# Split weight slabs of the gates: written to memory in the second token block, not in the first

## Chip, cores and metric

The kernel runs on one core of a Trainium2 chip. The metric is the device time of one launch in microseconds (us), given as the median of the runs that were made.

## The reference, cut to what matters

One layer of a streaming encoder. For 2048 prompt tokens and 64 sample tokens, with D_MODEL = 1024:

```python
h = rms_norm(x, norm1_g) * (1 + sc1) + sh1
z = h @ w_in                      # columns: glu_a, glu_b | q, k, v | g_conv, g_attn
u = glu_a * sigmoid(glu_b)
conv_out = swish(layer_norm(depthwise_conv31(u))) @ w_conv_out
attn_out = band_attention(rms_norm(q), rms_norm(k), v) @ w_attn_out   # 8 heads of 64
merged = sigmoid(g_conv) * conv_out + sigmoid(g_attn) * attn_out
x = x + gt1 * (merged @ w_o)
x = x + gt2 * swiglu_ffn(rms_norm(x, norm2_g) * (1 + sc2) + sh2)
```

The gates of this text are `g_conv` and `g_attn`: 2048 of the columns of `w_in`. All numbers are 32-bit floats.

## The kernel before, in words

**Products in three parts.** A 32-bit operand is split into a rounded part `hi`, a copy by the ScalarE (ACT) to the type float32r, and the rest `lo = src - hi`, a subtraction by the VectorE (DVE) or the GpSimd engine (POOL). `mm3` (L700) then makes three matmuls for each product: hi*hi, hi*lo and lo*hi. Weights have to be split as well. Their raw slabs are loaded into tiles named `wst`, their parts are the tiles `whi` and `wlo`.

**Two phases.** The first phase computes everything from `h` to the two mixers, in four blocks of tokens (`PBLOCKS`: 576 tokens, then three times 512). The second phase merges, projects and runs the FFN in three larger blocks. This text is about the first phase. There, for each block b, the stages follow in the order q, conv column 0, k, conv column 1, v, conv columns 2 and 3, g (`ORDER`, L553); the g stage computes the gates from 16 slabs of 512 rows by 256 columns, 512 KB each, in 8 pairs (`gates`, L1315). The key of such a slab is `("in", column, half)`, with three entries; the slabs of the conv columns have keys `("in", column)`, with two.

**Weights that come back.** The same weight slabs are needed in each of the four blocks. In block 0 a slab is loaded raw, split, and its two parts are stored to memory (`w_din_h`, `w_din_l`, 512 KB each, L501). In blocks 1 to 3 the two parts are loaded from there (L466). The first four slabs, those of q, are treated otherwise: block 0 doesn't store them (`passing`), and block 1 loads them raw once more, splits them and stores them.

**Who orders the work.** The class `Weights` keeps up to 5 split slabs (`held`) and, once opened, 3 raw ones (`staging`). `split` (L451) is called for the next slab as soon as an older one has been given back; `load` (L368) fetches the next raw slab as soon as a raw tile has been split. A small planner (`Stream`) adds up an estimated load of each engine and starts side work (norms of the next block, the attention heads, the convolution, its layer norm) in lanes between the matmuls, when their due times come. The framework then orders the instructions of each engine by its own estimate of when each can run. At run time each engine, and the SyncE queue (SP) that issues nearly all DMAs, works through its list in order.

**Engines in the first phase.** In block 0 DVE makes `wlo` for all slabs with `in` keys, POOL or DVE for others; in the second phase POOL makes most of them. DVE also runs the depthwise convolution, 31 taps as `y <- u, wd, y`, which lags behind the conv stages and reaches into the g stage of its block, and its part of the attention (`pr`, `sm`, `pl`). POOL runs sums of the layer norm (`s`, `y`), the reciprocal root (`r`) of the norms and small copies. The rows of the next block come as `x_t` (L1121), are squared by ACT (`junk`), scaled by DVE with POOL's `r`, and turned by the PE (`pt <- ident, x_t`) before the next block can begin on them.

Of the kernel before, what the change touches and what calls it, by code (L numbers as in the profile page):

```python
# [84 lines left out]
class Meter:  # L85


    def __init__(self, engine, name, stream):
        self.engine, self.name, self.stream = engine, name, stream
# [174 lines left out]
class Weights:  # L264
# [5 lines left out]
    def __init__(self, engines, pool, dram, stream, keys, source, staging, held, kept):  # L270
        self.stream = stream
        self.sync, self.act, self.dve, self.gps = engines
        self.pool, self.dram, self.keys, self.source = pool, dram, keys, source

        self.staging, self.held, self.reach = staging, held, 0
        self.sum_pool, self.sum_d, self.sums, self.hold, self.landed = None, None, {}, 0, {}
        self.behind = nullcontext

        self.room, self.leaving = {"wst": 1, "wup": 0, "wfo": 0}, {"wst": 0, "wup": 0, "wfo": 0}
        times, raws = {}, {}  # L280
        self.items, self.users, self.need, self.first, self.stored, self.spread = [], [], {}, set(), {}, set()

        def item(key):
            self.items.append(key)
            self.users.append(0)
            return len(self.items) - 1

        for i, key in enumerate(keys):
            n = times[key] = times.get(key, 0) + 1
            if key[0] == "up" and n == 1:  # L290
                self.first.add(i)
                cs = [c for f, op in key[1:] for c in self.columns_of(f, op)]
                for c in cs:
                    if c not in raws:
                        raws[c] = item(("fi", c))
                self.need[i] = sorted({raws[c] for c in cs})
                for f, op in key[1:]:
                    for c in self.parts_of(f, op):
                        self.users[raws[c]] += 1
            elif key[0] == "dn":  # L300
                fs = [key[:3], (*key[:2], key[2] + 1)]
                for f in fs:
                    if f not in raws:
                        raws[f] = item(("fo", f[2]))
                self.need[i] = [raws[f] for f in fs]
                for op in key[3:]:
                    for e in self.rows_of(op):
                        self.users[raws[fs[e]]] += 1
            elif n == 1 or not kept(key) or n == 2 and key[:2] == ("qkv", 0):
                self.need[i] = [item(key)]  # L310
                self.users[self.need[i][0]] += 1
                if key[0] == "fo" and key[1] in last_rows(0) and n == 1:
                    self.spread.add(self.need[i][0])
        self.raws = raws
        self.again = {key for key, n in times.items() if n > 1 and kept(key)}
        self.loaded, self.ready, self.used, self.freed, self.given = {}, [], 0, 0, 0

        self.extra = {"wst": staging - 1, "wup": 1, "wfo": 2}

        self.tags = {"fo": (), "": ("wst", "wup", "wfo")}  # L320
        self.due = {kind: [] for kind in self.tags}
        for i, key in enumerate(self.items):
            self.due[self.kind(key)].append(i)
        self.load_on("")
# [126 lines left out]
    def split(self):  # L451
        i = len(self.ready)
        key = self.keys[i]
        its = self.need.get(i, ())
        if key[0] == "dn":
            shape = [P, len(key) - 3, 512]
        elif i in self.first:
            shape = [P, 4 * len(key) - 4, P]
        else:
            shape = list(self.loaded[its[0]][0].shape) if its else self.stored[key][1]  # L460
        hi = self.pool.tile(shape, F32R, tag="whi", name="whi", bufs=self.held)
        lo = self.pool.tile(shape, F32R, tag="wlo", name="wlo", bufs=self.held)
        self.ready.append((hi, lo))
        if not its:
            for t, d in zip((hi, lo), self.stored[key][0]):
                self.sync.dma_start(t.bitcast(F32), d)  # L466
            return
        turn = {"wo": key[1], "fi": key[1] // P if key[0] == "fi" else 0}.get(key[0], 0)

        passing = key[:2] == ("qkv", 0) and i < 4  # L470
        on_dve = key[0] == "in" or key[0] == "qkv" and (passing or key[1]) or turn % 2
        if key[0] == "dn":
            parts = [(slice(j, j + 1), self.second(key, op)) for j, op in enumerate(key[3:])]
            self.stream.after("act", "pool")
        elif i in self.first:
            parts = [(slice(4 * j, 4 * j + 4), self.operand(f, op)) for j, (f, op) in enumerate(key[1:])]
            self.stream.after("act", "pool")
        else:
            n = 4 if key[0] == "fi" else shape[1]
            parts = [(slice(j, j + n), self.loaded[its[0]][0][:, j : j + n]) for j in range(0, shape[1], n)]  # L480
        for c, src in parts:

            late = key[0] in ("up", "fo") and self.stream.load["pool"] - self.stream.load["pe"] > POOL_BEHIND
            e, name = (self.dve, "dve") if on_dve or late else (self.gps, "pool")
            self.act.activation(hi[:, c], src, AF.Copy)
            self.stream.after(name, "act")
            e.tensor_tensor(lo[:, c], src, hi[:, c].bitcast(F32), ALU.subtract)
        if i in self.first:
            its = [self.raws[c] for f, op in key[1:] if op[0] == "a" for c in self.parts_of(f, op)]
        if key[0] == "dn":  # L490
            its = [self.raws[*key[:2], key[2] + int(op[1]) - 1] for op in key[3:] if op[0] == "b"]
        for j in its:
            self.drop(j, name)
        if key[0] == "dn" and key[3] == "b11":
            self.sum_second(key)

        def then():
            if key in self.again and key not in self.stored and not passing:
                ds = [self.dram.tile(shape, F32, name="w_d" + "_".join(map(str, key)) + "_" + part) for part in "hl"]
                for t, d in zip((hi, lo), ds):  # L500
                    self.sync.dma_start(d, t.bitcast(F32))  # L501
                self.stored[key] = ds, shape
            self.presum()

        self.stream.at(self.stream.when(name), then, True)

    def there(self, i):
# [56 lines left out]
def seven(s, f):  # L564


    return s > 0 and 2 <= f < NF - 2


def last_rows(s):  # L570

    return range(NF - (2 if s else 4), NF)


DOWN_OPERANDS = (("b11", "b21"), ("t3", "t2"), ("t1", "t4"), ("b22",))


def mod_order():
# [5 lines left out]
def weight_order():  # L584
# [10 lines left out]
    for s in range(len(CBLOCKS)):  # L595
# [4 lines left out]
        for f in range(0, NF, 2):  # L600
            ops = up_operands(f) + up_operands(f + 1)
            for j in range(0, len(ops), 2):
                yield ("up", *ops[j : j + 2])
                if f >= 2 and seven(s, f - 2):
                    yield from (("dn", s, f - 2, *DOWN_OPERANDS[i]) for i in {0: (0,), 2: (1, 2), 4: (3,)}.get(j, ()))
                elif j == 0 and f >= 2 and f - 2 not in last_rows(s):
# [5 lines left out]
def streaming_layer(ctx: ExitStack, tc: tile.TileContext, I, O):  # L612
# [1189 lines left out]
    for s, (lo, hi) in enumerate(CBLOCKS):  # L1802
# [215 lines left out]
        def down_pair(f):  # L2018
# [9 lines left out]
            def products(pss, a, w, j, first, last, i, e):  # L2028
                for p in range(n):
                    c = slice(p * P, p * P + P)  # L2030
                    mm3(pss[p], a[0][:, c], a[1][:, c], w[0][:, j], w[1][:, j], first, last, skip_group_check=True)
                    stream.after("dve", "pe")
                    dst = acc[p + i * n][:, 512 * e : 512 * e + 512]
                    dve.tensor_tensor(dst, dst, pss[p], ALU.add)

            w = W.get(("dn", s, f, *DOWN_OPERANDS[0]))
            products(ys, a11, w, 0, True, False, 0, 0)
# [3 lines left out]
            W.done()  # L2041
            w = W.get(("dn", s, f, *DOWN_OPERANDS[1]))
            products(zs, s3, w, 0, True, False, 1, 1)
            yield
            products(ys, s2, w, 1, False, False, 1, 0)
            W.done()
            w = W.get(("dn", s, f, *DOWN_OPERANDS[2]))
            products(ys, s1, w, 0, False, False, 1, 1)
            products(zs, a22, w, 1, False, True, 1, 0)
            W.done()  # L2050
            yield
            w = W.get(("dn", s, f, *DOWN_OPERANDS[3]))
            products(ys, s4, w, 0, False, True, 0, 1)
# [201 lines left out]
```

## Time and profile before

| | |
|---|---|
| median of 3 runs | 2989.11 us (2988.55 to 2995.56) |
| span of the profiled execution, first to last instruction | 2982.2 us |
| PE (matmul) busy | 2906.6 us, 97% |
| DVE, ACT, POOL busy | 2047.4, 1363.6, 1165.8 us (69%, 46%, 39%) |
| DMA, mean over the span | 211 GB/s |
| g stage of block 0, as far as its gate instructions show | about 195 to 332 us |
| g stage of block 1 | about 504 to 622 us |

The profile names no other time for its execution than the span; the median of the runs lies 6.9 us above it, which is what lies before the first and after the last instruction, and the difference between one execution and another. Times inside the span count from its first instruction. "Busy" of the PE counts overlapping matmuls, so a busy PE need not be at its peak. All lines of a helper carry its number, so that most instructions show L102; they are told apart by the names of their tiles.

### The profile page before, as it was taken

What the parts mean: (1) busy time and instruction counts of PE and PEld (TensorE: products, weight loads), DVE (VectorE), ACT (ScalarE), POOL (GpSimd) and SP (SyncE); (2) the same over time, 40 slices, a digit from 0 to 9 for tenths busy, and PEclk for the clock granted to TensorE, in tenths of its full rate; (3) what the DMA queues carried; (4) which work ended last, traced back from release to release, by engine and by line L of the source; (5) the groups of instructions that cost most, each with busy time, mean ns of one, the idle gap of its engine ahead of it and who ended that gap; (6) DMA issues with size and microseconds to landing.
All of it is one profiled execution on the core that took longest, in us unless ns stands there. A gap on an engine that the chain in (4) does not pass through costs nothing. (4 is left out here: it accounts for less than half of the span.)

```text
span 2982.2 us, 44930 instructions
## 1 busy us (share of the span) xinstructions
PE 2906.6 (97%) x16241; PEld 2588.0 (87%) x16241; DVE 2047.4 (69%) x3628; ACT 1363.6 (46%) x2459; POOL 1165.8 (39%) x752
## 2 busy tenths in 40 slices
PE   7999899999999999989999999999999999999999
PEld 4899777787888888878989899999999999999998
DVE  5897687667857885477677755676666557566666
ACT  3345643662456257464443335544444345444442
POOL 0201310111011102444666443365766742465767
PEclk9999999999999999999999999999999999999999
DMA  8989889888997888885444786423333975333333
GB/s 296 304 282 306 264 286 312 279 256 276 308 283 221 281 256 277 265 284 167 139 147 149 233 268 222 135 89 113 114 106 116 308 244 184 98 96 114 114 104 126
DMA packets 467724, 628.06 MB, mean 211 GB/s; under 512 B 36276, under 2 KB 314664, under 8 KB 467501
## 3 DMA queue, kind: packets, MB, share of 16 engines
q1 hardware_dynamic: 453456, 605.58, 62.8%
q10 hardware_dynamic: 14045, 19.60, 1.9%
q8 instruction: 128, 2.10, 0.3%
q14 instruction: 95, 0.78, 0.1%
HBM read 476.53 MB, written 148.54 MB: 210 GB/s over the span
## 5 line engine op out<-in xcount | busy, mean ns | idle before, releaser
L102 PE MATMUL ps<-t,whi 128*128 128x384 f32 (+1 forms) x2112 | 502.7, 322 | 9.5 <-ACT t L102 4.9
L102 POOL TENSOR_TENSOR wlo<-wst,whi 128x1024 fp32r<-128x1024 f32 (+1 forms) x160 | 365.1, 2292 | 254.1 <-ACT whi L102 231.9
L102 ACT ACTIVATE whi<-wst 128x1024 fp32r<-128x1024 f32 (+1 forms) x264 | 257.4, 977 | 324.8 <-PE ps L102 118.5
L102 PE MATMUL ps<-b,whi 128*128 128x384 f32 (+1 forms) x1584 | 381.3, 326 | 6.1 <-DVE early L102 3.4
L102 PEld LDWEIGHTS ps<-t,whi 128*128 128x128 f32 x2112 | 367.6, 188 | 17.2 <-ACT t L102 5.1
L102 DVE SCALAR_TENSOR_TENSOR y<-u,wd,y 128x512 f32<-128x512 f32 (+1 forms) x480 | 369.1, 773 | 6.4
L102 PE MATMUL ps<-hh,whi 128*128 128x512 f32 (+2 forms) x992 | 361.3, 364 | 0.0
L102 DVE TENSOR_TENSOR acc<-acc,pd 128x512 f32<-128x512 f32 (+1 forms) x482 | 322.5, 685 | 54.9 <-PE pd L102 52.4
L102 PE MATMUL ps<-hl,whi 128*128 128x512 f32 (+2 forms) x992 | 345.2, 348 | 0.0
L102 PE MATMUL ps<-hh,wlo 128*128 128x512 f32 (+2 forms) x992 | 344.9, 348 | 0.0
L102 PE MATMUL ps<-t,wlo 128*128 128x384 f32 (+1 forms) x1056 | 339.3, 321 | 1.0 <-POOL wlo L102 0.7
L102 PE MATMUL pd<-whi,hid 128*128 128x512 f32 (+1 forms) x956 | 307.2, 391 | 0.2 <-DVE hid L102 0.2
L102 PEld LDWEIGHTS ps<-b,whi 128*128 128x128 f32 x1584 | 278.6, 189 | 12.4 <-DVE early L102 4.2
L102 POOL TENSOR_TENSOR r<-t,mhalf 128x1 f32<-128x1 f32 (+3 forms) x68 | 83.7, 1232 | 456.4 <-DVE t L102 451.3
L102 PE MATMUL ps<-b,wlo 128*128 128x384 f32 (+1 forms) x792 | 256.9, 325 | 0.0
L102 ACT ACTIVATE pr<-pr,sm 128x640 f32<-128x640 f32 (+3 forms) x272 | 200.2, 747 | 109.7 <-DVE sm L102 107.1
L102 PEld LDWEIGHTS pd<-whi,hid 128*128 128x128 f32 (+1 forms) x956 | 174.6, 183 | 42.4 <-ACT hid L102 0.7
L102 PEld LDWEIGHTS ps<-hh,wlo 128*128 128x128 f32 x992 | 186.6, 188 | 21.7
L102 PEld LDWEIGHTS ps<-hh,whi 128*128 128x128 f32 x992 | 187.2, 189 | 18.5 <-issue 1.6
L102 PEld LDWEIGHTS ps<-hl,whi 128*128 128x128 f32 x992 | 187.3, 189 | 15.5 <-issue 1.4
L102 PEld LDWEIGHTS ps<-t,wlo 128*128 128x128 f32 x1056 | 198.2, 188 | 2.6 <-POOL wlo L102 1.3
L102 POOL TENSOR_TENSOR wlo<-ws,whi 128x512 fp32r<-128x512 f32 x96 | 125.2, 1325 | 173.7 <-ACT whi L102 170.8
(227 smaller groups left out, 6307.0 us busy)
## 6 DMA issues: line engine op xcount, KB each, us to landing
whi<-w_din_h SPq DMA_DIRECT2D x72, 512.0 KB, 6.6
wlo<-w_din_l SPq DMA_DIRECT2D x72, 512.0 KB, 8.2
wst<-sum_d SPq DMA_DIRECT2D x132, 256.0 KB, 2.8
wfo<-in_w_ffn_out SPq DMA_DIRECT2D x64, 512.0 KB, 3.3
wmod<-in_w_ada SPq DMA_DIRECT2D x46, 512.0 KB, 6.2
sum_d<-ws SPq DMA_DIRECT2D x88, 256.0 KB, 2.4
wst<-in_w_ffn_in SPq DMA_DIRECT2D x84, 256.0 KB, 3.1
wst<-in_w_in SPq DMA_DIRECT2D x40, 512.0 KB, 9.1
```

Of the source, the lines that this page charges most:

```text
L102: self.last = f(*args, **kw)
```

## The change

In block 0 the 16 gate slabs are loaded raw and split as before, with `lo` on DVE, but are not stored. In block 1 they are loaded raw again, split once more, now with `lo` on POOL, and the two parts are stored. Blocks 2 and 3 load the stored parts as before. The sets `unkept` and `anew` hold the positions in the list of weights of the first and of the later uses of these slabs.

```diff
@@ Weights.__init__
+        self.anew, self.unkept = set(), set()
...
         for i, key in enumerate(keys):
             n = times[key] = times.get(key, 0) + 1
+            if gate_slab(key):
+                (self.anew if n > 1 else self.unkept).add(i)
...
-            elif n == 1 or not kept(key) or n == 2 and key[:2] == ("qkv", 0):
+            elif n == 1 or not kept(key) or n == 2 and (key[:2] == ("qkv", 0) or gate_slab(key)):
                 self.need[i] = [item(key)]
@@ Weights.split
-        on_dve = key[0] == "in" or key[0] == "qkv" and (passing or key[1]) or turn % 2
+        on_dve = key[0] == "in" and i not in self.anew or key[0] == "qkv" and (passing or key[1]) or turn % 2
...
         def then():
-            if key in self.again and key not in self.stored and not passing:
+            if key in self.again and key not in self.stored and not passing and i not in self.unkept:
@@
+def gate_slab(key):
+
+    return key[0] == "in" and len(key) == 3
```

## The prediction

> **What bounds the kernel now.** I read the page first, then the busy time by windows of the two g stages, then who ended the waits of PE.
>
> ```profile
> PE 2906.6 (97%) x16241; PEld 2588.0 (87%) x16241; DVE 2047.4 (69%) x3628; ACT 1363.6 (46%) x2459; POOL 1165.8 (39%) x752
> ```
> ```profile
> core 0: us, PE busy (x) PEld busy (x) DVE busy (x) ACT busy (x) POOL busy (x), PEclk, DMA share, GB/s
> 195.00:332.00 137.00, 132.84 (x968) 127.64 (x967) 105.48 (x221) 81.22 (x182) 24.91 (x23) 1.00 0.86 282
> 504.00:622.00 118.00, 114.38 (x617) 96.56 (x616) 83.76 (x167) 70.75 (x130) 12.71 (x13) 1.00 0.90 286
> 504.00:549.00 45.00, 44.38 (x223) 36.80 (x221) 42.23 (x77) 21.94 (x39) 2.36 (x3) 1.00 0.89 281
> 549.00:622.00 73.00, 70.00 (x394) 59.76 (x395) 41.52 (x90) 48.80 (x91) 10.35 (x11) 1.00 0.91 288
> 352.70:360.00 7.30, 7.14 (x25) 5.53 (x26) 7.30 (x19) 3.97 (x7) 2.62 (x1) 0.59 0.69 161
> 450.00:500.00 50.00, 48.04 (x275) 37.17 (x274) 31.11 (x58) 12.87 (x24) 2.13 (x4) 1.00 1.02 320
> ```
>
> The first two windows are the g stages of block 0 and block 1. PE is 97% busy in both, at the full clock. Block 0, which loads raw slabs, splits them and stores the parts, loses no larger share than block 1, which only loads parts. So the stores that move are not what PE waits for in the stage itself. The waits say the same; first 195 to 360 us, then 504 to 640 us:
>
> ```profile
> PE pt L102 <- DVE x_t L102: 8.9, 4, 5.7
> PE pm L102 <- POOL s L102: 1.9, 1, 1.9
> ```
> ```profile
> PE pm L102 <- POOL s L102: 2.0, 2, 1.2
> PE sc L102 <- DVE sm L102: 1.6, 1, 1.6
> ```
>
> No gate slab and no DMA ends a wait of PE there. What stands out is the passage from block 0 to block 1, where PE waits four times, 8.9 us in all, for the rows `x_t` of the next block. Such a wait also halves the clock: after the longest of them the granted clock was 0.59 over 7.3 us (last window but one above), that is 0.41 * 7.3 = 3.0 us more. The kernel is bound by PE, and a change is worth what it adds to or takes from such waits: 8.9 + 3.0 = 11.9 us around block 0 at most.
>
> **The change, part by part.**
>
> *Block 0, stores gone.* Up to the end of block 0 the DMA list shows the stores and the raw loads:
>
> ```profile
> w_din_h<-whi SPq DMA_DIRECT2D x24, 512.0 KB, 5.6
> w_din_l<-wlo SPq DMA_DIRECT2D x24, 512.0 KB, 6.4
> ```
> ```profile
> ACT whi L102 <- DMA w_din_l<-wlo: 4.0, 1, 4.0
> ACT junk L102 <- DMA x_t<-in_x_prompt: 2.4, 1, 2.4
> ```
> ```profile
> 309.51 0.43 SPq L501 DMA_DIRECT2D w_din_l<-wlo  x1
> 338.92 1.11 SPq L1121 DMA_DIRECT2D x_t<-in_x_prompt  x1
> 352.74 1.09 PE L102 MATMUL pt<-ident,x_t 128*128 128x128 f32 x4 [5.65 <-DVE x_t L102]
> ```
>
> Of the 24 pairs 16 are the gates': 32 stores, 16.8 MB, go from the SP queue and the DMA engines. One wait of ACT for such a store (4.0 us) and one for the rows `x_t` (2.4 us) are what the trace puts down to DMAs here. ACT's 4.0 us don't reach PE by the waits above. The large wait of PE, 5.65 us at 352.74, hangs on a row load that SP issued at 338.92, 29 us after the last gate store; the stores can hardly have held it. So the gain lies between 0 and 11.9 us. I take **-2.4 us**, the one wait that a DMA ended and that stands ahead of the row transposes.
>
> *Block 1, splits on ACT and POOL.* The prices of one split:
>
> ```profile
> L102 ACT ACTIVATE whi<-wst 128x1024 fp32r<-128x1024 f32 x40 | 42.2, 1058 | 43.1 <-PE ps L102 24.2 <-DMA wst<-in_w_in 8.9 <-DMA gqk<-in_k_norm_g 4.3
> L102 POOL TENSOR_TENSOR wlo<-wst,whi 128x1024 fp32r<-128x1024 f32 x127 | 306.6, 2424 | 190.8 <-ACT whi L102 180.0 <-DMA x_t<-in_x_prompt 10.4 <-POOL wlo L102 0.2
> ```
>
> ACT gets 16 * 1.058 = 16.9 us on 70.75 of 118 us: 87.7. POOL gets 16 * 2.424 = 38.8 us on 12.71: 51.5. Both fit, so I price them at 0 by themselves. What covers them is the store of five split slabs: PE uses one in 118 / 16 = 7.4 us, so a slab is made some 4 * 7.4 = 29.5 us ahead. Without that cover each slab would cost 1.06 + 2.42 = 3.5 us. What is queued behind a late POOL is shown by its longest wait in this stage:
>
> ```profile
> POOL s L102 <- DVE y L102: 48.9, 2, 25.0
> ```
>
> A `wlo` behind a sum `s` that waits 25.0 us would be done after 25.0 + 2.4 = 27.4 us, just inside the 29.5. In turn a sum `s` behind a `wlo` is 2.4 us later, and PE's `pm` waits for that: 0 to 2 * 2.4 = 4.8 us; I take 0, since few of the sums meet a `wlo`.
>
> *POOL against DVE.* POOL is not free of DVE in this trace:
>
> ```profile
> 230.33 4.60 POOL L102 TENSOR_TENSOR s<-s,y 128x64 f32<-128x64 f32 x1 [32.54 <-DVE y L102]
> 266.66 0.30 POOL L102 TENSOR_TENSOR s<-s,y 128x64 f32<-128x64 f32 x1 [31.58 <-DVE y L102]
> ```
> ```profile
> 332.45 2.39 POOL L102 TENSOR_TENSOR wlo<-wst,whi 128x1024 fp32r<-128x1024 f32 x1 [8.58 <-ACT whi L102]
> 333.79 1.07 DVE L102 TENSOR_TENSOR ssq<-ssq 128x1 f32<-128x1 f32 x1 [0.53 <-ACT junk L102]
> 350.63 0.16 DVE L102 TENSOR_TENSOR ssq<-ssq 128x1 f32<-128x1 f32 x1 [2.14 <-ACT junk L102]
> ```
>
> The same small sum took 4.60 us under a dense run of convolution taps and 0.30 us later; and DVE's `ssq`, 0.16 us when alone, took 1.07 us beside a POOL `wlo` and ended with it (332.45 + 2.39 = 334.84, 333.79 + 1.07 = 334.86). Each seems to shut the other out for an instruction. Not every DVE instruction is hit: from 504 to 549 us, and in the second phase where POOL is busy,
>
> ```profile
> L102 DVE SCALAR_TENSOR_TENSOR y<-u,wd,y 128x512 f32<-128x512 f32 x44 | 31.6, 748 | 0.4
> ```
> ```profile
> L102 DVE TENSOR_TENSOR acc<-acc,pd 128x512 f32<-128x512 f32 x466 | 312.9, 685 | 54.9 <-PE pd L102 52.4
> L102 DVE TENSOR_TENSOR wlo<-ws,whi 128x512 fp32r<-128x512 f32 x64 | 68.3, 1078 | 11.4 <-ACT whi L102 9.5
> ```
>
> `acc`, which reads one PSUM operand, stays at 685 ns, while `wlo` of the same size, which reads two from SBUF, means 1078 ns. The taps `y <- u, wd, y` read two from SBUF and are 31.6 of DVE's 42.23 us between 504 and 549, a stretch of 45 us. Six slabs (45 / 7.4) are split in it, 6 * 2.424 = 14.5 us of POOL. If they shut out only the taps and run beside all the rest, the stretch needs 31.6 + 14.5 = 46.1 us, 1.1 too many; if they shut out all of DVE, 42.23 + 14.5 = 56.7 us, 11.7 too many. After 549 DVE has 73 - 41.5 = 31.5 us to spare and catches up. PE follows DVE through the scores (`sc <- DVE sm`), where it already waits 1.6 us. Ends: 0 (POOL gives way and its 29.5 us cover it) and 11.7. I take **+5 us**, nearer to the lower end, because of the `acc` row.
>
> [...]
>
> *DMA and SP in block 1.* 16.8 MB of loaded parts become 8.4 MB of raw loads and 16.8 MB of stores. Three raw slabs (1.6 MB) come earlier, so the stage moves 118 * 0.286 = 33.7 MB plus 6.8 = 40.5 MB. The DMA share would be 0.90 * 40.5 / 33.7 = 1.08, against 1.02 in the densest 50 us (450 to 500): 0.06 * 118 = 7 us too many at most. I take 0, since no DMA ends a wait of PE there now. SP issues 16 DMAs more; at 0.43 to 1.11 us each (rows above) that is 7 to 18 us in 118, beside work, and priced at 0. Its waits for `wlo` are a rival. Blocks 2 and 3 load what they loaded before: 0.
>
> **Sum.** -2.4 + 5.0 = +2.6 us on the span of 2982.2, so 2984.8. The median of the runs, 2989.11, lies 6.9 above the span; I add the sum to it: 2991.7, rounded **2992 us**.
>
> **The rivals.**
>
> *Faster: the passage to block 1 closes.* If lighter queues bring the rows early, the 11.9 us go; with DVE's cost at 1.1 that is -10.8: 2978 us. For it: SP and DMAs lose 16.8 MB just before. Against it: the 29 us between the last store and the load of the rows.
>
> *Slower: DVE is held up between 504 and 549 us.* The place is the run of taps; the price is 11.7 us late on DVE, plus 3.0 us of halved clock if PE's wait comes in one piece as at 352.74, less 2.4: +12.3, 3001 us. It decides from the point where POOL's 14.5 us hit more than DVE's taps, or where PE has no slack behind `sm`. For it: the 1.07 and 4.60 us rows, and 42.23 of 45 us busy. Against it: the `acc` row.
> [...]
>
> *Slower: SP stands behind POOL.* In block 1 a raw reload and the stores (L375, L501) wait in SP's list for `wlo`, and the attention's loads stand behind them.
>
> ```profile
> 515.97 1.08 SPq L1430 DMA_DIRECT2D bias<-rb_d  x2
> 526.84 0.81 DVE L102 CUSTOM_DVE_ANT_0 pr<-sc,bias 128x640 f32<-128x640 f32 x1
> bias<-rb_d SPq DMA_DIRECT2D x18, 144.0 KB, 4.1
> ```
>
> The bias is issued by 517.05, lands 4.1 us later and is used at 526.84: 5.7 us to spare. A stop of SP for POOL's whole 25.0 us would cost 25.0 - 5.7 = 19.3, less 2.4: 3006 us. Against it: that wait must fall on a `wlo`.
>
> *It doesn't do what it says:* the code leaves no room for that; each slab's second use has a raw item and a store.
>
> **How the numbers follow.** No change that matters (sum between -9 and +9) has 0.42; the faster rival 0.18; the DVE rival 0.30; the SP rival 0.10. 0.3% of the time, 9.0 us, is about what a measurement of this kernel can tell from no change. So faster 0.18, same 0.42, slower 0.40. The range goes from the faster rival, 2978, to the SP rival's 3006; what lies outside (waits of both passages together, or more than one stop of SP) I give 0.2. The likeliest case alone spans 2980 to 2998.
>
> **What would show it.** Right: no `w_din` store before 470 us, 32 after; 16 POOL `wlo` from about 470 to 600 us, longer than 2.4 us among the taps; DVE above 45 of 45 us worth of work between 504 and 549; PE's waits for `sm` in block 1 up from 1.6 us by some 5; the wait near 352 still there. Wrong: the `x_t` waits of 8.9 us gone (faster rival); PE waits for `whi` or `wlo` of the gates; waits of PE for a DMA of attention in block 1; or POOL and DVE side by side without stretching.

## The result and the profile after

The changed kernel took 3002.37 us (median of 5 runs, 2997.99 to 3004.37), the kernel before, run beside it, 2989.11 us (2982.78 to 2995.56). The ratio, which weighs all runs and isn't the quotient of the two medians, is 1.0038 with a 95% interval of 1.0022 to 1.0053. By the medians the kernel is slower by 13 us, where 2992 us, 3 more than before, had been forecast. The profiled execution took 3000.17 us with a span of 2998.4 us, 16.2 longer than that of before. In the runs measured since, a run's time lies 1.7 to 2.4 us above its span, so the traced execution of before took some 2984 us, 5 under its median; that of the changed kernel lies 2.2 under its own. So the traces overstate the difference of the medians by about 3 us.

The busy times of the page, and the windows of the two g stages as they were cut for the kernel before:

```profile
PE 2916.8 (97%) x16241; PEld 2594.1 (87%) x16241; DVE 2062.4 (69%) x3628; ACT 1376.5 (46%) x2475; POOL 1205.5 (40%) x768
```
```profile
195.00:332.00 137.00, 135.68 (x980) 130.28 (x979) 106.81 (x224) 84.53 (x195) 31.41 (x27) 1.00 0.71 213
504.00:549.00 45.00, 37.16 (x178) 30.18 (x179) 43.56 (x59) 21.47 (x36) 14.60 (x7) 0.96 0.78 246
549.00:622.00 73.00, 68.44 (x372) 58.30 (x372) 42.39 (x85) 43.37 (x75) 23.18 (x16) 0.95 0.86 277
```

Block 0 is better than before: PE 135.68 of 137 us instead of 132.84, the DMA share 0.71 instead of 0.86. Block 1 is far worse: PE 37.16 of 45 us instead of 44.38, and the clock is no longer full. The waits of PE (us in all, times, longest), 195 to 360 us and then 504 to 640 us:

```profile
PE sc L102 <- DVE sm L102: 2.6, 3, 1.4
PE pt L102 <- DVE x_t L102: 1.3, 1, 1.3
...
PE po L102 <- DVE pl L102: 6.0, 2, 5.3
PE sc L102 <- DVE sm L102: 3.9, 1, 3.9
PE ptp L102 <- ACT pr L102: 2.1, 2, 1.2
```

The waits for `x_t` fell from 8.9 to 1.3 us. In block 1 PE now waits for results of DVE in the attention, 6.0 us for `pl` and 3.9 us for `sm`.

How this adds up over the span is read from one more comparison: the start of the same ACT instruction in two traces. The table gives how much later it is than in the kernel before (us; minus is earlier), in the profiled execution of each kernel.

| in the trace of before at | 315.2 (end of g, block 0) | 363.6 (block 1 begun) | 504.6 (g, block 1) | 569.2 | 713.2 (block 2) | 1003.3 (block 3) | end |
|---|---|---|---|---|---|---|---|
| changed kernel | -5.8 | -12.6 | -12.7 | +2.6 | +10.2 | +15.0 | +16.2 |

So the change gains 12.6 us up to the start of block 1, and loses 23 from the g stage of block 1 to the start of block 2. Both are larger than the terms of the sum. Another 6 us are lost later; by what, stays open.

The loss in block 1 has two parts, waits and clock. The windows from 470 to 660 us, before and then after (the last three numbers of a row are the granted clock, the DMA share and GB/s):

```profile
470.00:540.00 70.00, 68.04 (x388) 54.23 (x387) 56.48 (x110) 30.41 (x55) 2.71 (x4) 1.00 0.95 298
540.00:600.00 60.00, 56.38 (x286) 46.10 (x285) 36.96 (x70) 36.37 (x63) 9.77 (x9) 1.00 0.90 270
600.00:660.00 60.00, 59.93 (x378) 53.31 (x377) 42.05 (x105) 38.88 (x79) 7.45 (x7) 1.00 0.77 242
```
```profile
470.00:540.00 70.00, 66.83 (x353) 53.58 (x353) 57.87 (x94) 35.47 (x61) 17.81 (x10) 0.98 0.90 285
540.00:600.00 60.00, 50.29 (x231) 40.85 (x231) 36.66 (x59) 32.29 (x51) 24.72 (x15) 0.91 0.81 259
600.00:660.00 60.00, 56.38 (x327) 48.32 (x326) 39.52 (x96) 34.30 (x71) 7.56 (x8) 0.94 0.89 283
```

PE is busy 173.5 us in place of 184.4, 11 us less. The clock falls short of full by 0.02 * 70 + 0.09 * 60 + 0.06 * 60 = 10.4 us, where it was full before. As an estimate, the two together are most of the 23 us: each microsecond that PE waits here cost about one more by the slower clock.

### The profile page after: what moved, and what is told of

Read it like the earlier page. It is cut to its first block, busy times and chain, and to the rows that moved or that the text cites. A ratio compares the mean times of both kernels' runs of the same rounds, so it can differ in the third digit from the quotient of the medians.

```text
span 2998.4 us, 44966 instructions
## 1 busy us (share of the span) xinstructions
PE 2916.8 (97%) x16241; PEld 2594.1 (87%) x16241; DVE 2062.4 (69%) x3628; ACT 1376.5 (46%) x2475; POOL 1205.5 (40%) x768
## 4 chain that ended last, share of the span: by engine, by line
PE 83%; DVE 7%; DMA 3%; ACT 2%; POOL 2%; issue 2%; SPq 0%; ACTq 0%; DVEq 0%; POOLq 0%
PE ps L102 54%; PE pd L102 15%; PE pw L102 6%; PE po L102 2%; PE sc L102 2%; DVE y L102 2%; PE ptp L102 2%; DVE wlo L102 2%; PE pt L102 1%; PE pa L102 1%; ACT whi L102 1%; DVE pw L102 1%; POOL wlo L102 1%; DMA x_t<-in_x_prompt 1%; DMA tg<-g_d 1%
## 5 line engine op out<-in xcount | busy, mean ns | idle before, releaser
L102 POOL TENSOR_TENSOR wlo<-wst,whi 128x1024 fp32r<-128x1024 f32 (+1 forms) x176 | 405.2, 2312 | 328.5 <-ACT whi L102 291.3
L102 ACT ACTIVATE whi<-wst 128x1024 fp32r<-128x1024 f32 (+1 forms) x280 | 274.1, 981 | 329.8 <-PE ps L102 119.3
L102 DVE SCALAR_TENSOR_TENSOR y<-u,wd,y 128x512 f32<-128x512 f32 (+1 forms) x480 | 382.8, 800 | 5.9
L102 PEld LDWEIGHTS ps<-t,whi 128*128 128x128 f32 x2112 | 367.8, 188 | 16.1 <-ACT t L102 5.2
L102 PEld LDWEIGHTS ps<-hl,whi 128*128 128x128 f32 x992 | 188.6, 190 | 16.8 <-issue 2.5
```

The source lines that it names most:

```text
L102: self.last = f(*args, **kw)
```

## Experiments

All times are medians against the kernel before on the same chip. It took 2988.71 us beside the block 0 half, the two with `lo` elsewhere and the last eight slabs; 2989.31 us beside the splits without stores, the stores without splits and the two kernels with the last four slabs; and 2988.88 us beside the thin stores, the stores on ACT and the two with the rows on ACT.

### Only the block 0 half

```diff
-                (self.anew if n > 1 else self.unkept).add(i)
+                n == 1 and self.unkept.add(i)
...
-            elif ... n == 2 and (key[:2] == ("qkv", 0) or gate_slab(key)):
+            elif ... n == 2 and key[:2] == ("qkv", 0):
...
+            if i in self.unkept and key != ("in", 2560, 0):
+                self.stored[key] = self.stored[("in", 2560, 0)]
```

> The half of the change in block 0 alone: of the gates only the first slab is stored in block 0, and blocks 1 to 3 load that one pair for each of the 16 slabs (same sizes, wrong gates), with no raw load and no split in block 1. If the missing stores are what brought block 1 forward by 14 us in the trace: 2975. If that was a chance of another order of instructions: 2985 to 2990.

Measured: 2977.05 us, ratio 0.9966 (0.9954 to 0.9979), which is 11.7 us less than before. The stores in block 0 are worth some 12 us (6 to 14 by the interval), as much as the whole passage in the faster rival, and not 2.4. What then remains for block 1 is 3002.37 - 2977.05 = 25 us.

### The lo of block 1 on DVE, and as a copy on ACT

```diff
-        on_dve = key[0] == "in" and i not in self.anew or ...
+        on_dve = key[0] == "in" or ...
```

> The changed kernel, but in block 1 DVE and not POOL makes the 16 wlo of the gates. [...] Theory of the queues (the added loads and stores of block 1 are what costs): nothing changes, 3002.

Measured: 2999.16 us, 1.0039 (1.0026 to 1.0051). This is not told apart from POOL's 3002.37, and by its number it fits the theory of the queues. The next kernel shows that `lo` has a price all the same.

```diff
+            if i in self.anew:
+                name = "act"
+                self.act.activation(lo[:, c], src, AF.Copy)
+            else:
...
```

> The changed kernel, but in block 1 the tiles wlo of the gates are a second copy by ACT and not the remainder, so that neither POOL nor DVE works for them; the gates of blocks 1 to 3 then hold wrong low parts, all loads, stores and matmuls are the same. [...] Queues: 3002, as the same DMAs run. A third possibility, that ACT becomes late by 16 * 1.06 = 17 us more work: 2985 to 2995 with waits of PE for ACT.

Measured: 2987.35 us, 0.9995 (0.9986 to 1.0004). 15 us less than the changed kernel: with the same slabs, stores and loads, but neither POOL nor DVE busy on `lo`. The groups of taps by shape (whole program; busy time, mean ns) of the kernel before, the changed one and the one with `lo` on ACT:

```profile
L102 DVE SCALAR_TENSOR_TENSOR y<-u,wd,y 128x512 f32<-128x512 f32 x360 | 268.2, 749 | 5.4
```
```profile
L102 DVE SCALAR_TENSOR_TENSOR y<-u,wd,y 128x512 f32<-128x512 f32 x360 | 281.5, 786 | 4.8
```
```profile
L102 DVE SCALAR_TENSOR_TENSOR y<-u,wd,y 128x512 f32<-128x512 f32 x360 | 268.1, 749 | 5.1
```

The taps took 281.5 - 268.2 = 13.3 us longer beside POOL, and nothing longer without it. In the changed kernel the stretch from 504 to 549 us alone holds 35 taps in place of 44:

```profile
L102 DVE SCALAR_TENSOR_TENSOR y<-u,wd,y 128x512 f32<-128x512 f32 x35 | 35.3, 1017 | 0.4
```

At the 748 ns of before they would have taken 26.2 us, so 9.1 us are lost there. With `lo` on DVE itself the taps take 269.2 us, and the price is another one: twelve of its `lo` lie between 470 and 600 us,

```profile
L102 DVE TENSOR_TENSOR wlo<-wst,whi 128x1024 fp32r<-128x1024 f32 x12 | 16.1, 1339 | 3.0 <-ACT whi L102 3.0
```

that is 16.1 us of DVE's own time, about as much as POOL takes from it. The changed kernel's timelines, POOL's and then DVE's, show how POOL takes it:

```profile
499.36 2.42 POOL L102 TENSOR_TENSOR wlo<-wst,whi 128x1024 fp32r<-128x1024 f32 x1 [14.05 <-ACT whi L102]
531.15 2.41 POOL L102 TENSOR_TENSOR wlo<-wst,whi 128x1024 fp32r<-128x1024 f32 x1 [4.58 <-ACT whi L102]
539.07 5.36 POOL L102 TENSOR_TENSOR wlo<-wst,whi 128x1024 fp32r<-128x1024 f32 x2 [5.50 <-ACT whi L102]
```
```profile
499.55 2.79 DVE L102 SCALAR_TENSOR_TENSOR y<-u,wd,y 128x512 f32<-128x512 f32 x1
531.27 2.84 DVE L102 SCALAR_TENSOR_TENSOR y<-u,wd,y 128x512 f32<-128x512 f32 x1
...
536.34 0.75 DVE L102 SCALAR_TENSOR_TENSOR y<-u,wd,y 128x512 f32<-128x512 f32 x1
537.13 7.85 DVE L102 SCALAR_TENSOR_TENSOR y<-u,wd,y 128x512 f32<-128x512 f32 x5
544.90 0.68 DVE L102 TENSOR_TENSOR pl<-ptp,ph 128x512 fp32r<-128x512 f32 x1
```

Two taps that began just behind a `wlo` ended only after it: 2.79 and 2.84 us in place of 0.75. Five taps took 7.85 us around the two `wlo` at 539.07, and the `pl` behind them, for which PE waits 5.3 us, came only at 544.90.

### Splits without stores, stores without splits

The first takes the 32 stores out of block 1, the second stores but neither loads raw nor splits:

```diff
 # splits, no stores: blocks 2 and 3 load the first slab's pair for all 16
...
+            if i in self.unkept and key != ("in", 2560, 0):
+                self.stored[key] = self.stored[("in", 2560, 0)]
...
```

> Left out: nothing of the gate slabs but the first pair is ever stored; blocks 2 and 3 load that pair for all 16 slabs. Block 1 loads the slabs raw and splits them (hi on ACT, lo on POOL) as the changed kernel does, without its 32 stores. Theory A (the price of block 1 is the split itself, POOL's lo standing in DVE's way and ACT's hi in the way of its other work): 2977.05 of the kernel with only the first half of the change, plus 12 to 15 for the lo as the runs with the lo elsewhere showed, plus up to 10 for the rest: 2990 to 3002. Rival B (the price is the 32 stores and what they do to SP's queue and the DMA engines): the raw loads move 8.4 MB less, so 2975 to 2982. If half and half: about 2989.

Measured: 2988.65 us, 1.0000 (0.9991 to 1.0009): 11.6 us above the kernel with only the block 0 half. Its taps are as slow as the changed kernel's:

```profile
L102 DVE SCALAR_TENSOR_TENSOR y<-u,wd,y 128x512 f32<-128x512 f32 x360 | 281.0, 784 | 5.0
```

So the split, with its raw loads, costs 11.6 us, and the stores on top of it the other half: 3002.37 - 2988.65 = 13.7 us. That is the time which the expectation gave for half and half. The stores alone (2975 to 2982) are ruled out; the split alone (2990 to 3002) is missed by 1.4 us, less than the 3 us that the interval leaves open. The two prices depend on the order in which they are taken: with the stores there, moving `lo` off POOL is worth 15.0 us (the kernel with `lo` on ACT), which leaves 10 for all the rest.

```diff
 # stores, no splits: the block 0 half, and in block 1
...
+            if i in self.back_at:
...
+                for t, d in zip((hi, lo), ds):      # the loaded parts, to memory that nobody reads
+                    self.sync.dma_start(d, t.bitcast(F32))
...
```

> Left out as in the kernel with only the first half of the change (one stored pair stands for all 16 slabs in blocks 1 to 3), but in block 1 the loaded parts are stored again, 32 stores of 0.5 MB from SP's queue to memory that nobody reads; nothing is loaded raw or split there. Theory A (the split is the price): 2977 to 2982. Rival B (the stores are the price): 2986 to 3002, with DMAs or SP ending waits of PE between 470 and 720 us, above all at the passage from block 1 to block 2. This kernel moves 8.4 MB more in block 1 than the changed one, so it rather overstates B.

Measured: 3017.3 us, 1.0096 (1.0082 to 1.0110), 40 us above the block 0 half and above both ranges. Of PE's waits from 470 to 720 us 6.3 us are now ended by a transfer of the attention (`kk <- k_d`). Stores cost time without any split, that much is clear; how much more they cost beside 16.8 MB of loads in place of 8.4 was not foreseen, and this kernel says nothing of their size in the changed one.

### What of the stores costs: the list or the bytes

```diff
 # a part of each store, at the same place of SP's list
...
+                thin = i in self.anew and key != ("in", 2560, 0)
                 for t, d in zip((hi, lo), ds):
+                    c = slice(0, 1 if thin else shape[1])
```

> The changed kernel with the 32 stores of block 1 issued as before, at the same places of SP's list and behind the same waits, but for 15 of the 16 slabs each store moves an eighth (64 KB in place of 512 KB); left out: the rest of those slabs, in whose place blocks 2 and 3 load the first slab's pair. The changed kernel is at 3002, the one without any of these stores at 2988.65. Theory A (the price is the bytes: the DMA engines are full in block 1 and SP waits for them): 2988 to 2992. Rival B (the price is SP's list: 32 more issues that wait for POOL's lo and hold up what stands behind them): 2998 to 3003.

Measured: 2996.79 us, 1.0021 (1.0011 to 1.0031). The part is not an eighth, as the expectation has it: the trace shows 15 of the 16 pairs of stores with 128 KB in place of 512, so a quarter of the bytes still moves.

```diff
-                    self.sync.dma_start(d, t.bitcast(F32))
+                    (self.act if i in self.anew else self.sync).dma_start(d, t.bitcast(F32))
```

> The changed kernel, with the stores of block 1 issued by ACT in place of SP; nothing is left out. Theory A (bytes): no change, 2999 to 3005, as the same bytes go at the same time, if ACT is not held up behind POOL. Rival B (SP's list): 2987 to 2994. If ACT waits for POOL's lo and holds its own work up: above 3005.

Measured: 2995.34 us, 1.0021 (1.0012 to 1.0031). Both lie between their two theories. From no stores to thin stores it is 8.1 us, from thin to whole 5.6; handing the issue to ACT gives 7.0 of 13.7 back. Each interval is about 3 us wide to either side, so the split of the 13.7 us is rough. If the price of the bytes goes by their number, the three quarters that are gone make 5.6 us, all of them 7.5, and the issues with their waits in SP's list the other 6.2: about half each, and which is larger isn't told apart. The waits of SP between 500 and 680 us, in the kernel before and then in the changed one, show the list from the inside:

```profile
SPq L466 <- PE ps L102: 42.1, 13, 9.5
```
```profile
SPq L504 <- DMA g_d<-gate: 27.9, 4, 8.6
SPq L469 <- PE ps L102: 9.5, 4, 8.4
```

Before, SP had time: it waited 42.1 us for PE to give back tiles, with the next load ready. Now that reserve is 9.5 us, and SP stands 27.9 us at the stores (L504); the profile names a transfer as what ended it, not POOL. But the lost reserve isn't the mark of the stores. The kernel that splits without them has still less of it, at 2988.65 us:

```profile
SPq L378 <- POOL wlo L102: 53.7, 9, 12.1
...
SPq L469 <- PE ps L102: 4.7, 4, 2.9
```

There SP stands 53.7 us at the raw loads (L378), which wait for POOL's `wlo`. So the raw loads alone take the reserve, and what the stores add is the 27.9 us at L504. Which of PE's waits those 27.9 us bring about, no run shows.

Something else has moved in block 1, the layer norm of the convolution. The last store of a convolution tile (`c_d`) that belongs to block 1, before and after, and the wait that follows it:

```profile
604.90 0.38 SPq L1311 DMA_DIRECT2D c_d<-part_h  x1
```
```profile
649.33 0.32 SPq L1319 DMA_DIRECT2D c_d<-part_h  x1
649.80 0.50 PE L102 MATMUL ps<-whi,hh 128*128 128x512 f32 x1 [2.17 <-ACT hh L102]
```

Before, the layer norm was done by 605 us, ahead of the passage to block 2. Now it runs until 649 us, together with the norms of the next block's rows on the same engines, and PE waits for `hh`. The split has moved it, not the stores. Its first scaling on ACT (`ln <- y,lnh`), at 569.65 us before, comes 33.3 us later in the changed kernel, 28.3 later in the one that splits without stores, 7.2 later in the one that stores without splits and 9.7 earlier with the block 0 half. Part of that is not delay but order: in ACT's list all four of these scalings stood ahead of the first `junk` of the next rows, and now three of the four stand behind it, with the stores and without. So the price of the split includes whatever this new order costs; no run has the splits in the old order.

### Fewer slabs

The change for the last eight slabs of sixteen, and for the last four:

```diff
-    return key[0] == "in" and len(key) == 3
+    return key[0] == "in" and len(key) == 3 and key[1] >= 2560 + 8 * P    # or 12 * P
```

> The change for the later 8 of the 16 gate slabs only; the first 8, split among the taps, are stored in block 0 and loaded as before. [...] Queues: half of the gain and half of the loss, 2993 to 2997.

Measured: 2990.71 us, 1.0009 (1.0000 to 1.0018), 2.3 us below the range of the queues. Its taps take 275.3 us, 7 more than before: the first three of its eight `wlo` (525 to 539 us) still lie among the taps, which end at 545 us.

> The change for the last four gate slabs of sixteen alone. With the last eight the time was that of before (2990.71 against 2988.71): a gain in block 0 paid back in block 1. Theory A (the gain hangs on the last stores ahead of the passage from block 0 to 1, the price on the taps of the convolution, each slab by itself some 1.5 us): the gain of 11 to 12 us mostly stays, and the price is 4 * 1.5 = 6: 2981 to 2985. Rival (gain and price both go by the number of slabs): a quarter of +13, with a quarter of -12: 2988 to 2991.

Measured: 2973.77 us, 0.9950 (0.9938 to 0.9963): faster than both kernels, by 15.5 us and 28.6 us. Its taps, and its waits of PE from 195 to 360 us:

```profile
L102 DVE SCALAR_TENSOR_TENSOR y<-u,wd,y 128x512 f32<-128x512 f32 x360 | 269.2, 752 | 5.3
```
```profile
PE pm L102 <- POOL s L102: 1.9, 1, 1.9
PE ptp L102 <- ACT pr L102: 1.3, 2, 1.2
PE pt L102 <- DVE x_t L102: 1.2, 1, 1.2
```

The four slabs come when the taps are over: the last tap of block 1 ends at 536 us, the first `wlo` begins at 558. The taps take 269.2 us against 268.2, so POOL takes 1 us from them instead of 13. And the `x_t` wait is as short as with all sixteen. Gain and price don't go by the number of slabs but by where they lie. The taps aren't the whole price, though: the four slabs by which the last eight differ from the last four cost some 17 us, of which the taps are 6; the rest stays open.

> The last four gate slabs are loaded raw and split in each of the four blocks and never stored: hi on ACT, lo on DVE in block 0 and on POOL in the later ones; 12 splits on POOL and 8 stores less than with the change for four slabs. Theory A (a lo on POOL at this end of the g stage costs about 1.5 us, stores at the end of block 1 little): three blocks pay 6 us each and block 0 gains up to 12: 2989 to 2997. Rival B (in the last quarter, behind the taps of the q, k and v convolution, POOL is out of DVE's way, and the lighter load traffic of 0.5 MB in place of 1.0 MB a slab helps): 2974 to 2982.

The edit lets only `gate_slab(key)` decide, in place of `n == 2` and `unkept`. Measured: 2983.43 us, 0.9980 (0.9971 to 0.9989), 9.7 us above the kernel that stores the four. Splitting three times instead of once costs more than 8 stores. The time lies 1.4 us above the second range, which is within the noise.

### The rows without the stores

If SP's list is what brought the rows late in the kernel before, then their load on another queue should help there:

```diff
-            ahead_x[t] = load_x(t, P, wa, "x", 3), ...
+            ahead_x[t] = load_x(t, P, wa, "x", 3, nc.scalar), ...
```

> The kernel before, with the loads of the rows x_t of the next block issued by ACT in place of SP; nothing is left out and the DMA engines move the same bytes. Theory A (in the kernel before, the last rows of block 1 come late because SP's list, in order and behind the stores, reaches their load only at 338.9 us): the load goes out some 10 to 20 us earlier, the wait of 5.65 us at 352.74 goes, and the time falls by 6 to 12: 2977 to 2983. Rival (the rows are late because the DMA engines are full, or the gain came from elsewhere in block 0): 2986 to 2992.

Measured: 2988.59 us, 0.9999 (0.9987 to 1.0010). At the place itself it did what was expected. The load of the last rows, in the changed kernel (from SP) and here (from ACT):

```profile
317.83 0.65 SPq L1129 DMA_DIRECT2D x_t<-in_x_prompt  x1
```
```profile
L1121 ACTq DMA_DIRECT2D x_t<-in_x_prompt x1: 339/339/339, 321.7 to 321.7; - x1
...
PE pt L102 <- DVE x_t L102: 1.3, 1, 1.3
```

It goes out at 317.83 and 321.7 us, against 338.92 in the kernel before, and PE's wait is 1.3 us in both. By the table's comparison this kernel is 6.9 us ahead at 363.6. But only 3.3 of it are left at 504.6, and at 1003.3 it is 2.1 us behind. So the runs show the place and the cause of that wait; that its removal alone shortens the kernel they don't show.

> The change for the last four gate slabs alone (2973.77), and the loads of the rows x_t of the next block issued by ACT; nothing is left out. Theory A (both take away the same wait at the passage from block 0 to 1): no further gain there, and a few us at the later passages: 2966 to 2975. Rival (the two gains have different causes and add): 2960 to 2966.

Measured: 2986.71 us, 0.9987 (0.9975 to 0.9998), 12.9 us above the change for four slabs. That is above both ranges: row loads from ACT take most of the gain away again. In its trace 7 of the 12.9 us are lost by 363.6 us, where it is 2.3 us ahead of the kernel before, against 9.3 for the four slabs alone. By what, stays open.

## Why the prediction was right and where it was wrong

The time lies in the range, and the sign of the sum was right; the likeliest case was no change that matters (within 0.3%), and the measured +0.38% (0.22 to 0.53) lies about at that bound. That it came out so near was in good part luck. The forecast of +2.6 us is the remainder of three terms that were all set too low, by 9, 7 and 14 us, and the first of these errors hides much of the other two. Measured: -12 (only the block 0 half), +11.6 (splits), +13.7 (stores of block 1), together +13; they are differences from one kernel to the next, so they add up by themselves, and each is good to some 3 to 4 us.

**Stores gone, -2.4: wrong, -12.** The step that failed is "the stores can hardly have held it". It compared the issue of the rows with the last store, 29 us earlier. But the load stands in one list with all that SP issues, and the stores had made the whole list later: before, the last row load was the 277th transfer that SP issued, in the changed kernel the 243rd, and it went out 21 us earlier (317.83 against 338.92). The choice between 0 and 11.9 us was made by which wait a DMA ended, which a late list doesn't show. The bound of 11.9 us came out in size, but not in its parts: it was all put at the passage, and of the 12.6 us in the trace 5.8 were won up to 315.2 us and 6.8 at the passage. "The wait near 352 still there" was wrong.

**POOL against DVE, +5: mechanism right, size wrong, 11.6.** The taps lost 13.3 us in all and 9.1 in the stretch from 504 to 549 us, for which the ends were 0 and 11.7. The `acc` row, by which +5 was taken, held: `acc` means 686 ns in the changed kernel too, against 685. But 31.6 of 45 us of DVE are taps, which were held up, and DVE was nearly full. The sum that led to the lower end (46.1 of 45 us) let the other instructions run while POOL holds up a tap; on DVE they stood behind the tap, as the `pl` at 544.90 behind five taps that took 7.85 us, and lost what it lost. PE paid through `pl` (6.0 us) and `sm` (3.9); the prediction named only `sm`. That POOL held up taps the trace shows, with 2.79 us in place of 0.75. That it holds up all of DVE, which gave the upper end of 11.7 us, the trace of the changed kernel contradicts: a `pl` begun at 507.76 us, within a `wlo` of POOL from 507.09 to 510.09, took 0.68 us, and the mean of all `pl` is 687 ns. The 11.6 us hold more than the lost time of the taps: `hi` on ACT, the raw loads and the new order of the layer norm are in them.

**DMAs and SP in block 1, 0 (up to 7): wrong, 13.7.** The step that failed is "I take 0, since no DMA ends a wait of PE there now". The premise was true and stayed nearly true after the change, but it doesn't bear a price of nothing: the kernels with and without these stores differ by 13.7 us, about half of it for the bytes and half for the issues and waits in SP's list, and SP stands 27.9 us at the stores. By which waits of PE the price is paid stays open. The rival in which SP stands behind POOL had a place that exists: without the stores SP waits 53.7 us for `wlo` at the raw loads. But its longest stop is 12.1 us and not 25.0, and in the changed kernel SP stands at the stores, where the profile names transfers. The DVE rival's 3001 us is closest to the result, but by a sum that lacks both the gain of 12 and the stores' 13.7.

**Splits on ACT and the covers, 0: not contradicted.** No wait of PE for a gate's `whi` or `wlo` appeared.

**The clock.** The likeliest case had no term for it, the DVE rival 3.0 us. Between 470 and 660 us the granted clock cost some 10 us; they are inside the prices above.

**The likeliest case had three terms that share one stretch.** They were added as if each had the slack to itself. With the upper ends, -11.9, +11.7 and +7, the sum would have been +6.8; the rest, some 6 us, is what the stores cost beyond the bound.

## What to carry to other kernels

A store that no engine waits for can still make what stands behind it in its queue's list later: with the stores of block 0 gone, a row load went out at 317.83 us in place of 338.92. Look at that list, and at the queue's own waits, before pricing a store at nothing. A lost reserve of the queue says that the next transfer can come late, not what that costs: here it was 9.5 us in a kernel of 3002 us and 4.7 in one of 2989. When work moves from one stage to another, price it by what the busiest engine does at that hour: four slabs behind the taps made them 1 us longer, sixteen, eleven of them ahead of the last tap, 13 us. And try the part before the whole: a quarter of this change gave -15.5 us, the whole +13.

## What was not expected of the hardware

The granted clock fell to 0.50 after waits much shorter than the 5.65 us of the kernel before. Two pairs of neighbouring windows of the changed kernel:

```profile
333.90:337.30 3.40, 1.35 (x7) 0.88 (x7) 2.70 (x9) 0.00 (x0) 0.70 (x2) 1.00 0.37 133
337.30:340.70 3.40, 3.30 (x8) 2.25 (x8) 1.92 (x8) 1.56 (x4) 1.50 (x1) 0.50 0.00 0
...
648.00:651.40 3.40, 1.58 (x10) 1.21 (x10) 2.05 (x7) 1.75 (x5) 2.17 (x2) 0.99 1.09 215
651.40:658.20 6.80, 6.17 (x19) 4.68 (x17) 4.36 (x11) 2.31 (x4) 1.95 (x1) 0.50 0.55 184
```

In the first window of each pair PE was busy for 1.35 and 1.58 of 3.40 us; its waits there were 1.3 us for `x_t` and 1.4 us for `sm` in the first pair, and 2.17 us for `hh` in the second. In the next 3.4 and 6.8 us the clock was 0.50. The prediction had a term for the clock only if PE's wait came in one piece, as the 5.65 us at 352.74. In the second pair the slower clock is up to 6.8 * 0.5 = 3.4 us, more than the 2.17 us wait itself. How busy PE must be to keep its clock is not shown: in the same trace the clock stayed at 1.00 after a window with 1.54 of 3.40 us busy (1327.2 to 1330.6; PE was busy for 2.47 of the next 3.40), and fell to 0.50 after one with 1.96 (1204.3 to 1207.7).
